# A state-space scan whose states are stored by half, chunk and run: neighbours in every step, real and imaginary rows swapped by ScalarE, four doubling steps in place of fifteen, single buffers

## The chip, the cores and the metric

One core of a Trainium2 chip runs the whole layer as one program. The metric is the device time of one execution, in microseconds (us); lower is better.

## What is computed

The reference is one hybrid decoder layer for 1024 positions of width 2048, all in 32-bit floats:

```python
h = rms_norm(x, norm_w)
q, k, v, a_gate, u, z, g_a, g_s = split(h @ w_in)
y_a = (sliding_window_attention(q, k, v, sinks) * silu(a_gate)) @ w_attn_proj
y_ssm = gelu(s5_ssm(u))                     # 64 groups of 16 channels, 64 complex states each
glu_a, glu_b = split(y_ssm @ w_glu + b_glu)
y_s = (glu_a * sigmoid(glu_b) * silu(z)) @ w_ssm_proj
x = x + (sigmoid(g_a) * y_a + sigmoid(g_s) * y_s) @ w_out
```

Inside `s5_ssm` a group's state follows s(t) = a s(t-1) + B u(t), with a complex diagonal a for each group, and y = Re(C s) + D u. This recurrence over 1024 positions is the scan that the change rewrites.

## The kernel before

Most of the program is matrix products on TensorE. Each weight tile of 128 x 1024 is loaded through SP's queue, split by ScalarE into a rounded high part `whi` and by VectorE into a rest `wlo` (`split`, lines 80 to 82), and used in `proj` (lines 110 to 127): 16 matmuls on `whi`, then 8 on `wlo`. These 24 matmuls are called a chunk below. The weight buffers `raw`, `whi` and `wlo` are two deep, so a late split of one chunk holds the loads and splits of the next ones.

Beside this main work run side jobs, written as Python generators. `drive` takes one step of the main job, then `pull` takes steps of the side jobs at a given rate. That fixes the program's order; a scheduler with its own timeline then sets the order of instructions on each engine, which is fixed when the program is built. Every engine works strictly through its own queue.

The scan is the side job `ssm` (lines 656 to 763), spawned at line 1180 beside the gate and sigmoid projections. 1024 positions are 128 blocks of 8, and the state is carried from block to block. Groups are taken in four batches of 16 (`bt`). In a batch:

- Loads bring the block inputs `uq` and the tables for B; GpSimd multiplies these into `bm` (lines 696 to 701), TensorE makes the block contributions `px` (line 706), and ScalarE copies them into `X` (line 708), once for each half `q` of 8 groups.
- `X` holds for every group 128 blocks and one zero in front. Real parts are in partitions 0 to 63, imaginary parts in 64 to 127. VectorE scans it with `step` (lines 713 to 725): one step is `xo += al*xi + be*swap(xi)`, and the swap of halves is made by two 64-row multiplications that read the other half (lines 722 and 723). So a step is five instructions.
- There are three parts. In 16 runs of 8 blocks, 7 steps go along each run, on 16 x 16 values whose neighbours lie 8 elements apart. Then 15 steps in sequence carry the run ends, on 16 values each. Then two steps spread each run's start over its 7 other blocks, 840 values each.
- GpSimd makes the output table `ct` (`ctable`, lines 438 to 452), `tz` is loaded, TensorE multiplies both with `uq` and `X` into `py` (lines 753 and 754), ScalarE applies GELU, and 16 stores write the result.

`uq`, `X`, `ct`, `c1`, `c2`, `v1` and `v2` have two buffers each, and `tz` one of its own, so that parts of the next batch can start while the present one is scanned. The power tables `p1`, `p2`, `al`, `be` are made in `ssm_prep` at the start and read once for all groups (lines 673 to 675).

The order of positions in a block row is set where `uproj` writes `ut` (lines 203 to 206), and undone in `glu` (line 959).

```python
tt(v1, xi, a, mul)
tt(v2[0:64], xi[64:128], b[64:128], mul)
tt(v2[64:128], xi[0:64], b[0:64], mul)
tt(v1, v1, v2, add)
tt(xo, xo, v1, add)
```

Of the kernel before, what the change touches and what calls it, by code (L numbers as in the profile page):

```python
# [32 lines left out]
def _build(nc, tc, I, OUT, ctx):  # L33
# [24 lines left out]
    PTD = dp.tile([4, 128, 9, NG], F32, name="ptd")  # L58
# [162 lines left out]
    for kt in range(KT):  # L221
# [5 lines left out]
        x = b0.tile([128, TH], F32, tag="x0", bufs=10, name="x0")  # L227
# [210 lines left out]
    def ctable(bp, tt, eng, p1, p2, g0, ng):  # L438

        shp = [128, ng, 9, 16]  # L440
        ct = bp.tile([128, 8, 9, 16], F32, tag="ct", bufs=2, name="ct")
# [1 line left out]
        c1 = bp.tile([128, ng, 16], F32, tag="c1", bufs=2, name="c1")
        c2 = bp.tile([128, ng, 16], F32, tag="c2", bufs=2, name="c2")
# [9 lines left out]
    def ssm_prep(bp, pp):  # L454
# [160 lines left out]
        al, be = tl((128, 9, NG), "al"), tl((128, 9, NG), "be")  # L615
# [40 lines left out]
    def ssm(bp, pp):  # L656
# [6 lines left out]
        def ts(o, a, s1, s2=None, op0=ALU.mult, op1=ALU.add):  # L663
            if s2 is None:
                V.tensor_scalar(o, a, s1, None, op0=op0)
            else:
# [4 lines left out]

        mul, add, sub = ALU.mult, ALU.add, ALU.subtract
        p1, p2, al, be = (tl((128, 9, NG), n) for n in ("p1", "p2", "al", "be"))
        for n, t in enumerate((p1, p2, al, be)):
            nc.sync.dma_start(t, PTD[n])
        for bt in range(4):
            gs = bt * GB
            uq = tl((128, GB, NCH), "uq", 2)
# [3 lines left out]
            X = tl((128, GB, NCH + 1), "X", 2)  # L682
            V.memset(X[:, :, 0:1], 0.0)

            for q in range(2):
# [16 lines left out]
                for qq in range(2):  # L702
# [5 lines left out]
                    S.copy(X[:, q * 8 + qq * 4:q * 8 + qq * 4 + 4, 1:NCH + 1], px)  # L708
                yield

            X4 = X[:, :, 1:NCH + 1].rearrange("p g (s k) -> p g s k", k=8)

            def step(xo, xi, a, b, shp):
                n = math.prod(shp)
                v1 = tl((128, 840), f"v1{bt % 2}")[:, 0:n]
                v2 = tl((128, 840), f"v2{bt % 2}")[:, 0:n]
                if len(shp) == 2:
                    v1, v2 = (v.rearrange("p (a b) -> p a b", a=shp[0]) for v in (v1, v2))
                elif len(shp) == 3:
                    v1, v2 = (v.rearrange("p (a b c) -> p a b c", a=shp[0], b=shp[1]) for v in (v1, v2))  # L720
# [587 lines left out]
```

## Time and profile before

| | |
|---|---|
| median of 3 runs (lowest to highest) | 2611.91 us (2608.07 to 2616.03) |
| the profiled execution, its span | 2613.01 us, 2611.2 us |
| TensorE matmuls busy | 2480.6 us, 95% of the span |
| VectorE busy | 1654.7 us, 63% |
| ScalarE busy | 916.9 us, 35% |
| GpSimd busy | 917.3 us, 35% |
| mean granted TensorE clock | 0.981 of full speed |

Shares of the whole span hide the stages. The scan lies between about 860 and 1460 us of the span, and it is read by windows of that stretch: for each window the busy time of each engine and the granted clock (1.00 is 2.4 GHz, 0.5 is 1.2 GHz).

### The profile page before, as it was taken

What the parts mean: (1) busy time and instruction counts of PE and PEld (TensorE: products, weight loads), DVE (VectorE), ACT (ScalarE), POOL (GpSimd) and SP (SyncE); (2) the same over time, 40 slices, a digit from 0 to 9 for tenths busy, and PEclk for the clock granted to TensorE, in tenths of its full rate; (3) what the DMA queues carried; (4) which work ended last, traced back from release to release, by engine and by line L of the source; (5) the groups of instructions that cost most, each with busy time, mean ns of one, the idle gap of its engine ahead of it and who ended that gap; (6) DMA issues with size and microseconds to landing.
All of it is one profiled execution on the core that took longest, in us unless ns stands there. A gap on an engine that the chain in (4) does not pass through costs nothing. (4 is left out here: it accounts for less than half of the span.)

```text
span 2611.2 us, 30785 instructions
## 1 busy us (share of the span) xinstructions
PE 2480.6 (95%) x11012; PEld 2016.8 (77%) x11012; DVE 1654.7 (63%) x2294; ACT 916.9 (35%) x1378; POOL 917.3 (35%) x715
## 2 busy tenths in 40 slices
PE   7999999999999998899999989999999999899997
PEld 5878887788878777787777868887877877678886
DVE  7995557984776287948586243226687686744542
ACT  5332454453666223131332232223352231233311
POOL 4110014350444534132120230004547656514466
PEclk9999999999999998999999999999999999999999
DMA  6543343223333745445464674336358677797765
GB/s 206 191 139 109 96 141 105 84 83 97 97 95 103 217 129 135 152 129 157 133 168 135 210 259 156 121 121 202 120 191 282 211 257 234 246 313 270 226 218 181
DMA packets 195609, 438.55 MB, mean 168 GB/s; under 512 B 41312, under 2 KB 53632, under 8 KB 195456
## 3 DMA queue, kind: packets, MB, share of 16 engines
q1 hardware_dynamic: 159680, 344.14, 43.6%
q0 software_dynamic: 19504, 63.08, 6.4%
q10 hardware_dynamic: 16272, 29.38, 2.9%
q8 instruction: 86, 1.41, 0.2%
q14 instruction: 67, 0.55, 0.1%
HBM read 341.73 MB, written 94.77 MB: 167 GB/s over the span
## 5 line engine op out<-in xcount | busy, mean ns | idle before, releaser
L121 PE MATMUL ps<-hh,whi 128*128 128x512 f32 x2144 | 851.3, 397 | 13.7 <-ACT whi L81 9.7
L122 PE MATMUL ps<-hl,whi 128*128 128x512 f32 x2144 | 844.5, 394 | 0.8 <-DVE hl L144 0.8
L82 DVE TENSOR_TENSOR wlo<-wraw,whi 128x1024 fp32r<-128x1024 f32 (+1 forms) x344 | 448.6, 1306 | 455.3 <-ACT whi L81 216.9
L125 PE MATMUL ps<-hh,wlo 128*128 128x512 f32 x2144 | 549.8, 396 | 32.0 <-DVE wlo L82 32.0
L81 ACT CAST whi<-wraw 128x1024 fp32r<-128x1024 f32 (+1 forms) x344 | 348.4, 1014 | 627.4 <-PE ps L122 301.3
L125 PEld LDWEIGHTS ps<-hh,wlo 128*128 128x128 f32 x2144 | 404.7, 190 | 124.6 <-DVE wlo L82 39.5
L121 PEld LDWEIGHTS ps<-hh,whi 128*128 128x128 f32 x2144 | 407.2, 190 | 108.5 <-ACT whi L81 17.1
L122 PEld LDWEIGHTS ps<-hl,whi 128*128 128x128 f32 x2144 | 407.1, 190 | 86.7 <-DVE hl L144 2.1
L82 DVE TENSOR_TENSOR wlo<-ws,whi 128x1024 fp32r<-128x1024 f32 x80 | 118.9, 1488 | 127.1 <-ACT whi L81 93.7
L81 ACT CAST whi<-ws 128x1024 fp32r<-128x1024 f32 x80 | 84.0, 1051 | 307.5 <-POOL ws L856 116.7
L856 POOL TENSOR_TENSOR ws<-wraw 128x512 f32<-128x512 f32 (+1 forms) x72 | 136.5, 1896 | 135.6 <-DVE wlo L82 103.3
L421 POOL TENSOR_TENSOR pa<-ph,c_mct 128x512 fp32r<-128x512 f32 x32 | 43.1, 1347 | 253.8 <-ACT ph L81 253.6
L178 POOL DMA_DIRECT2D gsd<-sg x32 | 17.5, 547 | 274.9 <-ACT sg L177 274.9
L177 ACT ACTIVATE sg<-sg 128x512 f32<-128x512 f32 x64 | 40.5, 632 | 198.1 <-DVE sg L176 198.0
L661 DVE TENSOR_TENSOR v<-X,be 64x16 f32<-64x16 f32 (+2 forms) x192 | 91.9, 479 | 2.8
L402 ACT ACTIVATE scs<-scs,m,rq 128x128 f32<-128x128 f32 x128 | 61.8, 484 | 63.9 <-DVE m L396 63.9
L1001 POOL TENSOR_TENSOR mt<-mt,pa 128x512 f32<-128x512 f32 x32 | 57.0, 1782 | 76.9 <-DMA pa<-pd 24.3
L178 POOL DMA_DIRECT2D gd<-sg x32 | 17.8, 556 | 170.6 <-ACT sg L177 163.5
L862 PE MATMUL psm<-q4h,whi 128*128 128x512 f32 x160 | 67.6, 422 | 4.0 <-DVE mt L996 2.7
L862 PE MATMUL psm<-q1h,whi 128*128 128x512 f32 x160 | 64.4, 403 | 6.1 <-ACT whi L81 6.1
L863 PE MATMUL psm<-q4l,whi 128*128 128x512 f32 x160 | 66.2, 414 | 0.0
L862 PE MATMUL psm<-q2h,whi 128*128 128x512 f32 x160 | 62.6, 392 | 3.1 <-ACT qa L893 3.1
(343 smaller groups left out, 4187.8 us busy)
## 6 DMA issues: line engine op xcount, KB each, us to landing
wraw<-w_in SPq DMA_DIRECT2D x268, 512.0 KB, 3.6
wraw<-w_out SPq DMA_DIRECT2D x72, 512.0 KB, 5.2
x<-xT SPq DMA_DIRECT2D x96, 256.0 KB, 4.0
gd<-sg POOLq DMA_DIRECT2D x32, 256.0 KB, 3.9
gsd<-sg POOLq DMA_DIRECT2D x32, 256.0 KB, 2.9
wraw<-w_glu SPq DMA_DIRECT2D x16, 512.0 KB, 4.3
wraw<-w_attn SPq DMA_DIRECT2D x16, 512.0 KB, 5.1
sga<-gd SPq DMA_DIRECT2D x32, 256.0 KB, 4.3
```

The lines of the kernel that those rows point to most:

```text
L81: S.copy(hi, src)
L82: V.tensor_tensor(lo, src if src2 is None else src2, hi.bitcast(F32), op=ALU.subtract)
L121: PE.matmul(ps, hi[:, kk, :], rh[kt], start=(kt == 0), stop=False)
L122: PE.matmul(ps, hi[:, kk, :], rl[kt], start=False, stop=False)
L125: PE.matmul(ps, lo[:, kk, :], rh[kt], start=False, stop=(kt == last))
L402: S.activation(sc[:, r, :], sc[:, r, :], AF.Exp, bias=m4[:, r:r + 1], scale=RQ[h, p][:, b, 2 * r + e:2 * r + e + 1], accum_out=den[:, r:r ...
L421: G.tensor_tensor(a, ph.bitcast(F32), mb, op=ALU.mult)
L661: (eng or V).tensor_tensor(o, a, b, op=op)
L856: G.tensor_tensor(o, a, b, op=ADD)
L862: PE.matmul(ps, hi[:, c0 + k, :], rh, start=(first and k == 0), stop=False, skip_group_check=True)
L863: PE.matmul(ps, hi[:, c0 + k, :], rl, start=False, stop=False, skip_group_check=True)
L1001: G.tensor_tensor(t, t, p, op=ADD)
```

## The change

Positions inside a half of 512 are reordered from (run and chunk, position) so that for a fixed chunk k of a run the 8 runs s of that half lie side by side. `X` becomes (group, half, 9 chunks, 8 runs); chunk 0 holds the state with which a run starts. `step` copies its input with the two halves of partitions exchanged into `xs` with two ScalarE copies, and VectorE then has four instructions over all 128 partitions. The run ends are gathered into `E`, and four steps with distances 1, 2, 4 and 8 replace the fifteen; for them `al` and `be` get three more powers, squared one from another in `ssm_prep`, which takes `x0` from 10 to 9 buffers. The power tables are loaded for each batch. `uq`, `X`, `ct`, `c1`, `c2`, `v1`, `v2` have one buffer; `tz` is loaded by halves into the buffer of `bm`, and `E` takes the buffer of `bmu`.

```diff
-            raw = b0.tile([128, TH], F32, tag="x0", bufs=10, name="ur")
+            raw = b0.tile([128, TH], F32, tag="x0", bufs=9, name="ur")
...
-            src = ps.rearrange("p (c j) -> p j c", j=8)
-            V.tensor_tensor(ut, src, rstd[h].rearrange("p (c j) -> p j c", j=8), op=ALU.mult)
+            order = lambda t: t.rearrange("p (s k j) -> p j k s", k=8, j=8)
+            V.tensor_tensor(ut.rearrange("p j (k s) -> p j k s", k=8), order(ps), order(rstd[h]), op=ALU.mult)
...
-        al, be = tl((128, 9, NG), "al"), tl((128, 9, NG), "be")
+        al, be = tl((128, 12, NG), "al"), tl((128, 12, NG), "be")
...
+        for n in (9, 10, 11):
+            p = slice(n - 1, n)
+            cmul(al[:, n:n + 1, :], be[:, n:n + 1, :], al[:, p, :], be[:, p, :], al[:, p, :], be[:, p, :],
+                 u1[:, 0:1, 0:NG])
...
-            uq = tl((128, GB, NCH), "uq", 2)
+            p1, p2, al, be = (tl((128, 9 if n < 2 else 12, GB), t) for n, t in enumerate(("p1", "p2", "al", "be")))
+            for n, t in enumerate((p1, p2, al, be)):
+                nc.sync.dma_start(t, PTD[n, :, 0:9 if n < 2 else 12, gs:gs + GB])
+            uq = tl((128, GB, NCH), "uq", 1)
...
-            X = tl((128, GB, NCH + 1), "X", 2)
+            X = tl((128, GB, 2, 9, 8), "X", 1)
...
-                tt(v1, xi, a, mul)
-                tt(v2[0:64], xi[64:128], b[64:128], mul)
-                tt(v2[64:128], xi[0:64], b[0:64], mul)
+                S.copy(m[0:64], xi[64:128])
+                S.copy(m[64:128], xi[0:64])
+                tt(v1, bc(xi), a, mul)
+                tt(v2, bc(m), b, mul)
                 tt(v1, v1, v2, add)
                 tt(xo, xo, v1, add)
...
-            for s in range(1, 16):
-                step(X4[:, :, s, 7], X4[:, :, s - 1, 7], al[:, 8, gs:gs + GB], be[:, 8, gs:gs + GB], (GB,))
+            E = tl((128, GB, 1, 16), "bmu", name="E")
+            S.copy(E.rearrange("p g o (h s) -> p (g o) h s", h=2), X[:, :, :, 8, :])
+            for n, d in enumerate((1, 2, 4, 8)):
+                bc = lambda x: x[:, 8 + n, :].unsqueeze(2).unsqueeze(3).to_broadcast([128, GB, 1, 16 - d])
+                step(E[:, :, :, d:16], E[:, :, :, 0:16 - d], bc(al), bc(be), (GB, 1, 16 - d))
+            S.copy(X[:, :, 0, 0, 1:8], E[:, :, 0, 0:7])
+            S.copy(X[:, :, 1, 0, :], E[:, :, 0, 7:15])
...
-            tz = tl((128, GB, 128), "tz", 1)
+                tz = tl((128, 8, 128), "bm", 1, name="tz")
...
-                G.tensor_tensor(o.rearrange("p (c i) -> p i c", i=8), g.rearrange("p (i c) -> p i c", i=8),
-                                z.rearrange("p (c i) -> p i c", i=8), op=MUL)
+                back = lambda t: t.rearrange("p (s k i) -> p i k s", k=8, i=8)
+                G.tensor_tensor(back(o), g.rearrange("p (i k s) -> p i k s", i=8, k=8), back(z), op=MUL)
```

How the built order moves is shown at three places. The first is VectorE in the steps along the runs of the first batch, from one weight split to the next (L82 is the split, L661 and L665 are the scan, `v` is `v1` or `v2`). Before:

```order
L82 TENSOR_TENSOR wlo<-wraw,whi 128x1024
L661 TENSOR_TENSOR v_7552<-X,al 128x256
L661 TENSOR_TENSOR v_7553<-X,be 64x256 x2
L661 TENSOR_TENSOR v_7552<-v_7552,v_7553 128x256
L661 TENSOR_TENSOR X<-X,v_7552 128x16x16
L661 TENSOR_TENSOR v_7589<-X,al 128x256
L661 TENSOR_TENSOR v_7590<-X,be 64x256 x2
L661 TENSOR_TENSOR v_7589<-v_7589,v_7590 128x256
L82 TENSOR_TENSOR wlo<-wraw,whi 128x1024
```

Now:

```order
L82 TENSOR_TENSOR wlo<-wraw,whi 128x1024
L665 TENSOR_TENSOR v_7613<-X,al 128x256
L665 TENSOR_TENSOR v_7614<-xs,be 128x256
L665 TENSOR_TENSOR v_7613<-v_7613,v_7614 128x256
L665 TENSOR_TENSOR X<-X,v_7613 128x32x8
L665 TENSOR_TENSOR v_7657<-X,al 128x256
L665 TENSOR_TENSOR v_7658<-xs,be 128x256
L665 TENSOR_TENSOR v_7657<-v_7657,v_7658 128x256
L665 TENSOR_TENSOR X<-X,v_7657 128x32x8
L82 TENSOR_TENSOR wlo<-wraw,whi 128x1024
```

About two steps stand between two weight splits in both; a step has four instructions in place of five.

The second is ScalarE in the same stretch (L81 makes `whi`, L705 copies `px` into `X`, L715 and L716 are the swaps, L177 is a sigmoid). Where before only L81 and L177 stand there, it is now:

```order
L705 COPY X<-px 128x8x64 x2
L715 COPY xs<-X 64x256
L716 COPY xs<-X 64x256
L81 CAST whi<-wraw 128x1024
L715 COPY xs<-X 64x256
L716 COPY xs<-X 64x256
L177 ACTIVATE sg<-sg 128x512
L715 COPY xs<-X 64x256
L716 COPY xs<-X 64x256
L81 CAST whi<-wraw 128x1024
```

Each cast of a weight tile now stands behind one or two pairs of swaps, and each pair waits for VectorE's step before it.

The third is GpSimd where the first batch ends and the second begins (`ct`, `ctu`: output table; `bm`, `bmu`: input table; L193 issues a store). Before:

```order
L661 TENSOR_TENSOR ct<-ct,ctu 128x1152
L661 TENSOR_TENSOR ctu<-c_10294,p_7277 128x1152
L661 TENSOR_TENSOR bm<-pwr,bre 128x8x64
L661 TENSOR_TENSOR bm<-pwr,bim 128x8x64
L661 TENSOR_TENSOR bm<-bm,bmu 128x8x64
L661 TENSOR_TENSOR bmu<-pwi,bre 128x512
L661 TENSOR_TENSOR bm<-bm,bmu 128x8x64
L193 DMA agd_75<-sg 128x512
```

Now:

```order
L665 TENSOR_TENSOR bm<-pwr,bre 128x8x64
L665 TENSOR_TENSOR bm<-pwr,bim 128x8x64
L665 TENSOR_TENSOR ct<-c_9031,p_8212 128x1152
L665 TENSOR_TENSOR bm<-bm,bmu 128x8x64
L665 TENSOR_TENSOR ct<-ct,ctu 128x1152
L193 DMA agd_75<-sg 128x512
L665 TENSOR_TENSOR bmu<-pwi,bre 128x512
L665 TENSOR_TENSOR ctu<-c_9117,p_8213 128x1152
L665 TENSOR_TENSOR bm<-bm,bmu 128x8x64
```

All of the rows shown second wait for the last `py` product of the first batch, since `tz` sits in the buffer of `bm`.

## Rows read from the trace of the kernel before

**Rows 1.** Who TensorE waited for, 860 to 1460 us: total, times, longest.
```profile
PE ps L125 <- DVE wlo L82: 29.3, 14, 4.8
PE px L706 <- POOL bm L661: 13.0, 2, 6.5
```
**Rows 2.** Busy time by stretch: PE, PEld, DVE, ACT, POOL, granted clock, DMA share, GB/s.
```profile
860.00:1415.00 555.00, 505.90 (x2282) 413.50 (x2281) 390.52 (x656) 151.55 (x181) 159.76 (x114) 0.96 0.54 151
900.00:925.00 25.00, 21.86 (x96) 18.69 (x97) 8.80 (x6) 6.54 (x8) 23.77 (x15) 0.86 0.71 226
925.00:1005.00 80.00, 73.12 (x329) 58.33 (x328) 73.98 (x139) 17.24 (x21) 16.09 (x13) 0.98 0.35 111
1030.00:1060.00 30.00, 23.48 (x99) 19.63 (x98) 23.20 (x27) 7.92 (x9) 13.04 (x9) 0.83 0.79 203
1060.00:1130.00 70.00, 61.41 (x252) 48.76 (x251) 62.20 (x127) 14.56 (x17) 9.58 (x12) 0.95 0.46 143
1300.00:1330.00 30.00, 25.97 (x122) 21.03 (x122) 16.94 (x19) 12.55 (x19) 13.35 (x8) 0.89 0.74 170
1570.00:1640.00 70.00, 70.00 (x310) 57.98 (x310) 20.39 (x21) 18.00 (x20) 4.27 (x8) 1.00 0.43 143
```
**Rows 3.** VectorE's groups by form, 860 to 1460 us: busy, mean ns of one.
```profile
L82 DVE TENSOR_TENSOR wlo<-wraw,whi 128x1024 fp32r<-128x1024 f32 x89 | 128.8, 1448 | 155.2 <-ACT whi L81 91.6 <-PE ps L125 52.4 <-DMA c<-sC 7.0
L661 DVE TENSOR_TENSOR v<-X,be 64x256 f32<-64x256 f32 x56 | 44.3, 790 | 0.8
L661 DVE TENSOR_TENSOR v<-X,be 64x840 f32<-64x840 f32 x16 | 26.6, 1661 | 0.4
L661 DVE TENSOR_TENSOR X<-X,v 128x256 f32<-128x256 f32 x28 | 22.3, 797 | 0.8
L661 DVE TENSOR_TENSOR v<-X,be 64x16 f32<-64x16 f32 x120 | 21.1, 176 | 1.7
L661 DVE TENSOR_TENSOR v<-X,al 128x256 f32<-128x256 f32 x28 | 20.5, 732 | 7.1 <-ACT X L708 6.5
...
L661 DVE TENSOR_TENSOR v<-v,v 128x256 f32<-128x256 f32 x28 | 14.2, 506 | 0.6
L661 DVE TENSOR_TENSOR v<-X,al 128x840 f32<-128x840 f32 x8 | 12.9, 1614 | 0.2
...
L661 DVE TENSOR_TENSOR X<-X,v 128x840 f32<-128x840 f32 x8 | 8.2, 1030 | 0.2
```
**Rows 4.** VectorE in order of time: start, length; the same addition twice.
```profile
932.62 1.34 DVE L661 TENSOR_TENSOR v<-v,v 128x256 f32<-128x256 f32 x1
...
939.68 0.43 DVE L661 TENSOR_TENSOR v<-v,v 128x256 f32<-128x256 f32 x1
```
**Rows 5.** GpSimd in order of time, the same microseconds.
```profile
932.12 1.56 POOL L661 TENSOR_TENSOR bm<-pwr,bim 128x512 f32<-128x512 f32 x1
...
937.14 1.46 POOL L661 TENSOR_TENSOR bm<-bm,bmu 128x512 f32<-128x512 f32 x1
```
**Rows 6.** ScalarE's groups by form: small and cross-partition copies, up to 1640 us.
```profile
L404 ACT ACTIVATE es<-es 128x4 f32<-128x4 f32 x32 | 6.1, 190 | 0.0
...
L312 ACT CAST kh<-kk 64x512 fp32r<-64x512 f32 x4 | 2.5, 618 | 0.1
```
**Rows 7.** GpSimd's groups by form, 860 to 1640 us.
```profile
L661 POOL TENSOR_TENSOR bm<-bm,bmu 128x512 f32<-128x512 f32 x16 | 25.4, 1587 | 0.5
L661 POOL TENSOR_TENSOR ct<-ct,ctu 128x1152 f32<-128x1152 f32 x8 | 21.6, 2694 | 0.4
L661 POOL TENSOR_TENSOR ctu<-c,p 128x1152 f32<-128x1152 f32 x8 | 21.0, 2627 | 0.4
```
**Rows 8.** VectorE's groups by form, whole span: a product with broadcast operands.
```profile
L459 DVE TENSOR_TENSOR ct<-c,p 128x1152 f32<-128x1152 f32 x8 | 10.7, 1342 | 0.0
```
**Rows 9.** Busy time by stretch, 100 to 200 us.
```profile
100.00:200.00 100.00, 100.00 (x496) 79.91 (x495) 93.23 (x131) 31.89 (x42) 14.16 (x24) 1.00 0.47 145
```
**Rows 10.** The product with z in the GLU: count, least, median and greatest ns, first and last start.
```profile
L959 POOL TENSOR_TENSOR s<-ga,z x16: 1651/2049/2123, 1815.3 to 1957.9; 128x512 f32<-128x512 f32 x16
```

More of the change, by code (lines that the diff above doesn't have):

```diff
@@ L57, in _build @@
     PWD = dp.tile([2, 8, NG, 64], F32, name="pwd")
-    PTD = dp.tile([4, 128, 9, NG], F32, name="ptd")
+    PTD = dp.tile([4, 128, 12, NG], F32, name="ptd")
     KD = dp.tile([16, NG, 256], F32, name="kd")
@@ L226, in _build @@
             w[n, 1] = load_w(win(12 + n)[1], 2, *spare[n])
-        x = b0.tile([128, TH], F32, tag="x0", bufs=10, name="x0")
+        x = b0.tile([128, TH], F32, tag="x0", bufs=9, name="x0")
         nc.sync.dma_start(x, I["xT"][kt, :, 0:TH])
@@ L435, in attention_block, with ctable @@
         yield
[L438 removed]
+    def ctable(bp, tt, eng, p1, p2, g0, ng, at, bufs):
         shp = [128, ng, 9, 16]
[L441 removed]
+        ct = bp.tile([128, 8, 9, 16], F32, tag="ct", bufs=bufs, name="ct")
         u = bp.tile([128, 8, 9, 16], F32, tag="ctu", bufs=1, name="ctu")
[L443 to L444 removed]
+        c1 = bp.tile([128, ng, 16], F32, tag="c1", bufs=bufs, name="c1")
+        c2 = bp.tile([128, ng, 16], F32, tag="c2", bufs=bufs, name="c2")
         nc.sync.dma_start(c1, I["sC1"][:, g0:g0 + ng, :])
@@ L707, in ssm @@
                                   uq[:, q * 8 + gg, :], start=True, stop=True)
-                    S.copy(X[:, q * 8 + qq * 4:q * 8 + qq * 4 + 4, 1:NCH + 1], px)
+                    S.copy(X[:, q * 8 + qq * 4:q * 8 + qq * 4 + 4, :, 1:9, :].rearrange("p g h k s -> p g h (k s)"),
+                           px.rearrange("p g (h c) -> p g h c", h=2))
                 yield
-            X4 = X[:, :, 1:NCH + 1].rearrange("p g (s k) -> p g s k", k=8)
             def step(xo, xi, a, b, shp):
                 n = math.prod(shp)
[L715 to L720, printed above, removed]
-                tt(v1, xi, a, mul)
-                tt(v2[0:64], xi[64:128], b[64:128], mul)
-                tt(v2[64:128], xi[0:64], b[0:64], mul)
+                v1, v2 = (tl((128, 896), t)[:, 0:n].rearrange("p (a b c) -> p a b c", a=shp[0], b=shp[1])
+                          for t in ("v1", "v2"))
+                m = tl((128, 256), "xs")[:, 0:math.prod(xi.shape[1:])]                     .rearrange("p (a b c) -> p a b c", a=shp[0], b=xi.shape[2])
+                S.copy(m[0:64], xi[64:128])
+                S.copy(m[64:128], xi[0:64])
+                bc = lambda x: x if x.shape[2] == shp[1] else x.to_broadcast([128] + list(shp))
+                tt(v1, bc(xi), a, mul)
+                tt(v2, bc(m), b, mul)
                 tt(v1, v1, v2, add)
@@ L735, in ssm @@
-            for q in range(2):
-                shp = [128, 8, 15, 7]
-                gl = slice(q * 8, q * 8 + 8)
-                bc = lambda x: x.rearrange("p k g -> p g k")[:, gs + q * 8:gs + q * 8 + 8, 1:8] \
-                    .unsqueeze(2).to_broadcast(shp)
-                step(X4[:, gl, 1:16, 0:7], X4[:, gl, 0:15, 7:8].to_broadcast(shp), bc(al), bc(be), shp[1:])
-                yield
-            tz = tl((128, GB, 128), "tz", 1)
-            for j in range(8):
-                nc.sync.dma_start(tz[16 * j:16 * j + 16], KD[:, gs:gs + GB, 128 - 16 * j:256 - 16 * j])
@@ L746, in ssm @@
-            for q in range(2):
-                ct = ctable(bp, tt, G, p1, p2, gs + q * 8, 8)
+            E = tl((128, GB, 1, 16), "bmu", name="E")
[3 more added lines that the diff above has]
+                step(E[:, :, :, d:16], E[:, :, :, 0:16 - d], bc(al), bc(be), (GB, 1, 16 - d))
+                if n % 2:
+                    yield
@@ new lines, in ssm @@
+            S.copy(X[:, :, 0, 0, 1:8], E[:, :, 0, 0:7])
+            S.copy(X[:, :, 1, 0, :], E[:, :, 0, 7:15])
+            for h in range(2):
+                bc = lambda x: x.rearrange("p k g -> p g k")[:, :, 1:8].unsqueeze(3).to_broadcast([128, GB, 7, 8])
+                step(X[:, :, h, 1:8, :], X[:, :, h, 0:1, :], bc(al), bc(be), (GB, 7, 8))
+                yield
+            for q in range(2):
+                tz = tl((128, 8, 128), "bm", 1, name="tz")
+                for j in range(8):
+                    nc.sync.dma_start(tz[16 * j:16 * j + 16],
+                                      KD[:, gs + q * 8:gs + q * 8 + 8, 128 - 16 * j:256 - 16 * j])
+                ct = ctable(bp, tt, G, p1, p2, gs + q * 8, 8, q * 8, 1)
```

31 lines of the change are left out of this document (10 added, 21 removed).

## The prediction
> **What bounds the kernel now.** I read the stretch of the scan, not the page's shares. Over 860 to 1415 us TensorE's matmuls are busy 505.9 of 555 us and the granted clock averages 0.96 [rows 2]; so 49.1 us are idle and 0.04 x 555 = 22.2 us go to the lower clock level, 1.2 GHz. The list of TensorE's waits says for whom [rows 1]: 29.3 us, in 14 pieces, for VectorE's weight split `wlo`, and 13.0 us, in two pieces of 6.5, for GpSimd's input table `bm`. The rest is small.
>
> Why a weight split is late is read from the windows. From 925 to 1005 us, the first batch's scan, VectorE is busy 74.0 us [rows 2]. TensorE loses 80 - 73.1 = 6.9 us to idling and 0.02 x 80 = 1.6 to the clock, so its matmuls needed 71.5 us. VectorE had more to do than TensorE (103%). From 1060 to 1130 it is 62.2 us against 70 - 8.6 - 3.5 = 57.9 (107%). Two-deep weight buffers hide the first microseconds of such a lag; then TensorE waits once per chunk. **In the scan VectorE is the bound; elsewhere TensorE is.**
>
> I call the two places where a batch begins joints. They show the same wait and then a slower clock: in 900 to 925 us 0.14 x 25 = 3.5 us and in 1030 to 1060 us 0.17 x 30 = 5.1 us go to the clock [rows 2]. With the two waits of 6.5 us [rows 1] the joints cost 10.0 and 11.6 us, together 21.6. The window 1300 to 1330 us, where inputs are rebuilt, takes 0.11 x 30 = 3.3 us of clock loss and stays as it is. What is left of the clock loss, 22.2 - 3.5 - 5.1 - 3.3 = 10.3 us, belongs to the waits on `wlo`. **The scan costs 29.3 + 10.3 = 39.6 us.**
>
> **VectorE's scan.** Before, one step along the runs costs 0.732 + 2 x 0.790 + 0.506 + 0.797 = 3.62 us and there are 28: 101.2 us. The chain over run ends is 60 steps of five instructions of about 0.176: 52.8 us. The spread is eight steps of 1.614 + 2 x 1.661 + 2 x 1.030 = 7.00 (the sum of the two products, not shown, taken as the last addition): 56.0 us [rows 3]. Together 210 us.
>
> After, every instruction covers 128 partitions and reads runs of eight neighbours. Rows bound the price. Elements that lie 8 apart make the 128x256 addition 0.797 us; the contiguous one is 0.506, and at 840 elements in runs of seven neighbours it is 1.030, 1.2 ns per element where the former is 3.1 [rows 3]. Broadcast operands do not slow a product: 1152 elements in 1.342 us, 1.2 ns each [rows 8]. So I take the contiguous price, 0.506 at 256 elements and 0.0009 us for each further one. Steps along runs: 28 x 4 x 0.506 = 56.7 us. Doubling steps have 240, 224, 192 and 128 elements, 196 on average, 0.453 us: 16 x 4 x 0.453 = 29.0. Spread, 896 elements, 1.08: 8 x 4 x 1.08 = 34.6. Together 120 us, **90 us less**. If all went at the strided price it would be about 28 x 4 x 0.797 + 16 x 4 x 0.797 + 8 x 4 x 1.66 = 193 us, 17 less; that is the upper bound.
>
> There is a lower one. The same 128x256 addition took 1.34 us at 932.6, while GpSimd was multiplying tables, and 0.43 at 939.7, after GpSimd's last one had ended at 938.6 [rows 4, 5]. In the new order the tables of the next batch stand at the joint and no longer in the scan. At 0.43 the steps along runs cost 48.2 us, the doubling steps 24, and all about 105.
>
> The Trainium skill (SBUF — State Buffer, "Who interferes with whom") says that a VectorE instruction with two inputs in SBUF and a GpSimd instruction that reads SBUF take turns on one read interface. By that rule the forecast would be the fourth case below, with the scan at 0.43; the two rows agree with it.
>
> **What the swaps add.** ScalarE gets 104 swaps (two for each of 28 + 16 + 8 steps) and 12 copies around `E`. No row shows a 64x256 copy between halves; a 64x512 one takes 0.618 and a 4-element instruction 0.190 [rows 6]. In between lie 0.40 at 256, 0.36 at 196 and 0.30 at 128: 56 x 0.40 + 32 x 0.36 + 16 x 0.30 + 12 x 0.40 = 44 us (22 to 72 at the ends). ScalarE is busy 151.6 of 555 us [rows 2], so the room is there. What counts is order: VectorE waits for the second swap, having only the first product (0.51) to do meanwhile: 0.80 - 0.51 = 0.3 us for each of 52 steps, 16 us. Behind a waiting swap stand the casts that make `whi` (second excerpt of the order); they can come late by what is left of VectorE's step, some 1.4 us, and a weight buffer gives more than that.
>
> So a batch's scan takes (120 + 16) / 4 = 34 us of VectorE's time in place of 52.5. In the first batch that leaves 74.0 - 22.5 + 4 = 55.5 us, and since the scan now runs beside some ten chunks instead of thirteen or fourteen, about four weight splits fewer fall into it: near 49 us. A chunk needs 24 x 70.0 / 310 = 5.4 us of TensorE [rows 2], ten need 54. The load falls from 103 to about 91%. Two thirds of the scan's cost should go; I keep a third, 13 us, since the splits still stand behind two steps each. **Gain 27 us** (bounds: nothing, and all 39.6).
>
> **What single buffers add.** The next batch's `bm` may start only when the last `py` product has read `tz`. From there to `px` GpSimd has five table products of `bm`, two of `ct` and one of `ctu` (third excerpt, nine rows): 5 x 1.59 + 2 x 2.69 + 2.63 = 16.0 us [rows 7], and an issue of a store. The scheduler left 83 matmuls between them, 83 x 0.226 = 18.7 us. That holds by a little; I take 3 us for each of the three later joints. The first has no predecessor and stays at 10.0. Between the two halves of a batch `tz` is loaded again and `ct` made again: 2 us in each of four batches. `py` now waits for the end of a shorter scan right behind it: 1 us in each. Sum 10 + 9 + 8 + 4 = 31 us, against 21.6: **9 us lost**. No row of before shows the last two. Their bounds are nothing and the 6.5 us wait [rows 1] each time.
>
> **Costed at nothing.** Three more squarings in the preparation, 18 instructions, at most 18 x 0.506 = 9 us of VectorE, in a stretch where TensorE never idles [rows 9]; VectorE is busy 93% there, so if that cover went, some of the 9 us would show. Nine `x0` buffers: the last input tile's matmuls move behind 16 others that are ready earlier. The table loads are 12 more transfers, the `tz` loads 32 more, on SP's queue, where each weight load stands behind them; they fall into the joint terms. The product with z reads and writes with a wider stride, 2.05 us now [rows 10]; sixteen of them at 0.797 / 0.506 of that would add 19 us to GpSimd, which is not the bound there. After the scan the order of all engines is otherwise the same, so I expect the same times there.
>
> **Sum.** 2613.0 (profiled) - 27 + 9 = 2595. The median of the runs is 1.1 lower: **2594 us**.
>
> **The rivals.** *The gain is eaten.* Swaps slower than 0.4 us, or products at the strided price, leave VectorE at 100% and over in the scan: of 39.6 us some 30 stay, and with 9 lost at the joints it comes to 2612. For: the price of a swap is interpolated. Against: ten chunks leave 5 us of room.
>
> *Slower.* The later joints decide. If GpSimd's chain there exceeds 18.7 us, because it stands behind a store that waits for a late gate product, TensorE runs dry as in 1030 to 1060: 11.6 us each time instead of 3, also at the four reloads of `tz`. Seven times 11.6 is 81, plus the first 10.0, against 21.6: 70 lost, 27 gained, 2655; with half of them 2618 to 2635. For: exactly this wait stands there twice in the present trace. Against: 2.7 us of room.
>
> The Trainium skill (Trainium Kernel Development and Optimization, "Best Practices") advises double buffers so that transfers overlap with work. By that rule this case would be the likeliest; the two waits of 6.5 us arose with double buffers, so they do not bear it out.
>
> *Larger gain.* The scan free of GpSimd's tables at 0.43 and joints that hold: 2613.0 - 39.6 - 11.6 = 2562, less 1.1: 2561.
>
> **Chances.** Forecast 0.58 (2578 to 2603), larger gain 0.12, eaten 0.17, slower 0.13. A measurement of this kernel tells 0.3%, about 8 us, from no change; so faster means under 2604, slower over 2620. The range runs from 2564, into the larger gain, to 2619, over the eaten one, and leaves out the slower case and the end of the larger. Faster 0.71, same 0.17, slower 0.12.
>
> **What would show it.** Right: VectorE's scan near 120 us in four forms of about 0.45 to 0.5 and 1.1 us; TensorE's wait on `wlo` in this stretch under 15 us; its waits on `bm`, `tz` and `X` near 20. Wrong: products at 0.73 or more, swaps at 0.6, or waits of 5 us at every joint; or a gain that comes from outside 860 to 1460 us.

## The result and the profile after

The changed kernel takes 2546.29 us (median of 4 runs, 2542.53 to 2552.07), the kernel before on the same chip 2609.99 (2606.82 to 2616.03): a ratio of 0.9755, interval 0.9728 to 0.9783. It is faster by 64 us where 18 were forecast, and its time lies 18 us under the forecast range.

The profiled execution's span fell from 2611.2 to 2540.8 us. Busy time by stretch shows where (us; PE, PEld, DVE, ACT, POOL, granted clock, DMA share, GB/s). The kernel before, from the start of the stage to the same piece of work behind it (3873 and 3868 matmuls):

```profile
0.00:860.00 860.00, 836.07 (x3810) 675.10 (x3811) 629.06 (x966) 416.39 (x749) 252.79 (x225) 0.99 0.38 120
...
860.00:1785.00 925.00, 863.22 (x3873) 708.24 (x3871) 512.50 (x782) 252.99 (x300) 223.58 (x192) 0.97 0.53 158
```

The changed kernel:

```profile
0.00:860.00 860.00, 839.52 (x3814) 676.94 (x3815) 629.99 (x985) 418.00 (x749) 253.99 (x226) 0.99 0.38 120
...
860.00:1719.00 859.00, 842.19 (x3868) 700.17 (x3866) 413.01 (x509) 297.02 (x412) 227.04 (x192) 0.99 0.56 170
...
1719.00:2541.00 822.00, 777.49 (x3332) 630.00 (x3332) 514.52 (x548) 248.73 (x332) 440.47 (x299) 0.98 0.69 231
```

The preparation takes as long as before. The stage is 66 of the 70 us shorter: TensorE idles 16.8 us instead of 61.8, and its matmuls take 842.2 instead of 863.2 us, because the clock averages 0.99 instead of 0.97.

Who TensorE waited for from 860 to 1720 us in the changed kernel (total, times, longest), beside [rows 1]:

```profile
PE px L703 <- POOL bm L665: 9.3, 5, 3.4
PE ps L121 <- ACT whi L81: 4.7, 3, 4.2
PE ps L125 <- DVE wlo L82: 1.7, 1, 1.7
PE ps L122 <- DVE hl L144: 1.0, 1, 1.0
```

The waits for `wlo` are gone but for one of 1.7 us, and the single buffers did not lengthen those for `bm`. VectorE's and ScalarE's groups by form, 860 to 1400 us, beside [rows 3, 6]:

```profile
L82 DVE TENSOR_TENSOR wlo<-wraw,whi 128x1024 fp32r<-128x1024 f32 x88 | 130.3, 1481 | 147.0 <-PE ps L125 87.5 <-ACT whi L81 39.5 <-DMA yd<-yt 16.6
...
L665 DVE TENSOR_TENSOR X<-X,v 128x256 f32<-128x256 f32 x28 | 11.9, 423 | 0.8
L665 DVE TENSOR_TENSOR v<-v,v 128x256 f32<-128x256 f32 x28 | 11.8, 423 | 0.7
L665 DVE TENSOR_TENSOR v<-xs,be 128x256 f32<-128x256 f32 x28 | 11.8, 423 | 12.8 <-ACT xs L716 12.7
...
L665 DVE TENSOR_TENSOR v<-X,al 128x896 f32<-128x896 f32 x8 | 11.0, 1380 | 0.1
```
```profile
L715 ACT COPY xs<-X 64x256 f32<-64x256 f32 x28 | 11.4, 407 | 20.2 <-DVE X L665 19.8
```

An operation of a run step costs 0.423 us; VectorE's scan takes 106.0 us in all, 210.8 before.

The rows that explain the result are VectorE's weight splits (L82) inside the four batches' scans, from a scan's first operation to its last (us; DVE busy, count; clock, DMA share, GB/s). Before:

```profile
929.00:1002.00 73.00, 13.07 (x9) 0.98 0.31 102
1042.00:1120.00 78.00, 13.48 (x11) 0.94 0.48 153
1182.00:1254.00 72.00, 12.26 (x10) 0.96 0.44 138
1327.00:1402.00 75.00, 14.64 (x12) 0.98 0.52 141
```

In the changed kernel:

```profile
921.00:967.00 46.00, 9.76 (x8) 1.00 0.51 146
1033.00:1083.00 50.00, 10.98 (x9) 1.00 0.58 161
1148.00:1195.00 47.00, 11.42 (x9) 1.00 0.52 146
1262.00:1319.00 57.00, 12.21 (x10) 1.00 0.56 178
```

TensorE uses up a split in 5.42 us (24 matmuls, [rows 2]). Before, 42 splits stand in 298 us: 70 us more than the 228 that they feed. Now 36 stand in 200 us and feed 195. I call this difference the excess of a window.

A window is also stretched by the waits that fall into it, so its excess alone does not tell cause from effect. VectorE's busy time does. The sums over the same four windows, all instructions, before and in the changed kernel:

```profile
sum 298.00, PE 266.20 PEld 211.50 DVE 283.07 ACT 59.41 POOL 45.76; mean PE 66.55 PEld 52.87 DVE 70.77 ACT 14.85 POOL 11.44
```
```profile
sum 200.00, PE 199.97 PEld 165.05 DVE 169.01 ACT 98.52 POOL 13.80; mean PE 49.99 PEld 41.26 DVE 42.25 ACT 24.63 POOL 3.45
```

Before, VectorE worked 283 us beside splits that feed TensorE for 228; now it works 169 us beside splits that feed it for 195.

### The profile page after: what moved, and what is told of

Same layout as the page of the kernel before. It is cut to its first block, busy times and chain, and to the rows that moved or that the text cites. A ratio compares the mean times of both kernels' runs of the same rounds, so it can differ in the third digit from the quotient of the medians.

```text
span 2540.8 us, 30817 instructions
## 1 busy us (share of the span) xinstructions
PE 2459.2 (97%) x11012; PEld 2007.1 (79%) x11012; DVE 1557.5 (61%) x2040; ACT 963.8 (38%) x1492; POOL 921.5 (36%) x715
## 5 line engine op out<-in xcount | busy, mean ns | idle before, releaser
L82 DVE TENSOR_TENSOR wlo<-wraw,whi 128x1024 fp32r<-128x1024 f32 (+1 forms) x344 | 445.2, 1295 | 488.9 <-PE ps L125 247.7
L81 ACT CAST whi<-wraw 128x1024 fp32r<-128x1024 f32 (+1 forms) x344 | 349.8, 1018 | 637.2 <-PE ps L122 372.0
L125 PE MATMUL ps<-hh,wlo 128*128 128x512 f32 x2144 | 542.0, 391 | 1.7 <-DVE wlo L82 1.7
L81 ACT CAST whi<-ws 128x1024 fp32r<-128x1024 f32 x80 | 84.2, 1054 | 292.5 <-POOL ws L855 80.4
L82 DVE TENSOR_TENSOR wlo<-ws,whi 128x1024 fp32r<-128x1024 f32 x80 | 116.4, 1456 | 115.7 <-ACT whi L81 74.4
L178 POOL DMA_DIRECT2D gsd<-sg x32 | 17.8, 556 | 226.7 <-ACT sg L177 214.8
L177 ACT ACTIVATE sg<-sg 128x512 f32<-128x512 f32 x64 | 40.6, 634 | 136.5 <-DVE sg L176 136.4
L402 ACT ACTIVATE scs<-scs,m,rq 128x128 f32<-128x128 f32 x128 | 62.2, 487 | 61.9 <-DVE m L396 61.8
L1000 POOL TENSOR_TENSOR mt<-mt,pa 128x512 f32<-128x512 f32 x32 | 56.3, 1762 | 74.9 <-DMA sgs<-gsd 22.6
L178 POOL DMA_DIRECT2D gd<-sg x32 | 17.7, 555 | 177.7 <-ACT sg L177 165.3
L862 PE MATMUL psn<-q3l,whi 128*128 128x512 f32 x160 | 62.8, 393 | 1.6 <-DVE q3l L82 1.6
```

Of the source, the lines that this page charges most:

```text
L81: S.copy(hi, src)
L82: V.tensor_tensor(lo, src if src2 is None else src2, hi.bitcast(F32), op=ALU.subtract)
L125: PE.matmul(ps, lo[:, kk, :], rh[kt], start=False, stop=(kt == last))
L402: S.activation(sc[:, r, :], sc[:, r, :], AF.Exp, bias=m4[:, r:r + 1], scale=RQ[h, p][:, b, 2 * r + e:2 * r + e + 1], accum_out=den[:, r:r ...
L862: PE.matmul(ps, hi[:, c0 + k, :], rl, start=False, stop=False, skip_group_check=True)
L1000: G.tensor_tensor(t, t, p, op=ADD)
```

## The experiments

The kernel before was measured again with every set of experiments and took 2610 to 2614 us each time; ratios and their intervals are against it. The changed kernel's 0.9755 of that is 2546 to 2550. Theory A, at first: TensorE loses in proportion to VectorE's scan time. Waits are counted over the whole stage, where those for `wlo` were 32.0 us before. Three dots stand for lines left out of an edit.

**The swaps by VectorE again.**

```diff
-                S.copy(m[0:64], xi[64:128])
-                S.copy(m[64:128], xi[0:64])
...
-                tt(v2, bc(m), b, mul)
+                tt(v2[0:64], bh(xi[64:128]), b[64:128], mul)
+                tt(v2[64:128], bh(xi[0:64]), b[0:64], mul)
```

The sign in the table `be` moves to its other half with this.

> The changed kernel, but the halves are swapped by VectorE again: the product with be is two products of 64 partitions, and ScalarE's two copies per step are gone. VectorE's scan work goes from 106.0 us to about 132 (28 more of 0.42 us, 16 more of 0.29 to 0.40, 8 more of 1.09). Theory A (what TensorE loses in the stage follows VectorE's scan time, 61 us for the 104.8 that it fell by, so 0.58 us per us): 15 us slower than the changed kernel, 2561 us. Theory B (VectorE has slack and only above a threshold does it lose): within 5 us of the changed kernel, 2543 to 2551. Theory C (the gain came from the rearranged ends of the batches, their buffers and tables, not from VectorE's time): 2546 too, waits on wlo as few as now.

Measured 2551.08 us, 0.9751 (0.9728 to 0.9775), with VectorE's scan at 134.2 us: 28 us more work, at no cost that shows. The swaps on ScalarE brought nothing that shows. Theory A's straight line, which asked for 15 us, falls.

**A chain of 15 in place of doubling.**

```diff
-            for n, d in enumerate((1, 2, 4, 8)):
...
-                step(E[:, :, :, d:16], E[:, :, :, 0:16 - d], bc(al), bc(be), (GB, 1, 16 - d))
...
+            for s in range(1, 16):
...
+                step(E[:, :, :, s:s + 1], E[:, :, :, s - 1:s], bc(al), bc(be), (GB, 1, 1))
```


> The changed kernel, but the four doubling steps are a chain of 15 steps over one column each (16 elements per partition). VectorE's scan work goes up by about 20 us (23 out, 240 operations of 0.18 in = 43), ScalarE gets 88 more copies, and each batch's chain is some 10 us longer. Theory A (0.58 us per us of VectorE): 12 us slower, 2558 us. Theory B (threshold): 2543 to 2551. Theory D (it is the length of the chain, through the order of the joints, that counts, not the load): batches' joints later by 10 us each, 2560 to 2585 with waits of TensorE on px, py or X rather than on wlo.

Measured 2559.12 us, 0.9788 (0.9762 to 0.9813), some 9 us slower than the changed kernel. Waits for `wlo` 1.4 us, for `bm` 15.1 (9.3 there), for `whi` 9.5 (4.7). VectorE's load (127.2 us) does not make the splits late; the longer chain costs mostly at the joints, a little less than theory D asked for. The time alone would fit theory A as well (2558); the waits do not.

**X strided, same order.**

```diff
-            X = tl((128, GB, 2, 9, 8), "X", 1)
+            X = tl((128, GB, 2, 8, 9), "X", 1).rearrange("p g h s k -> p g h k s")
```

ScalarE's copy of `px` into `X` becomes two copies with this, one for each half.

> The changed kernel with the same instructions of VectorE in the same order, but X is laid out so that a step's states lie 9 elements apart instead of side by side. The run steps' two operations that touch X go from 0.42 us to 0.73 and 0.80 (rows of the kernel before), so VectorE's scan work rises by about 21 us to 127. If the price of a stride is the reason for the cheaper steps, X<-X,v of 256 is again near 0.80 us here; if not, it stays at 0.42. Time by theory A: 12 us slower, 2558; by B or C: 2543 to 2551.

Measured 2568.52 us, 0.9831 (0.9798 to 0.9865). Some 19 us slower, but not for the reason expected. VectorE's and TensorE's groups by form:

```profile
L665 DVE TENSOR_TENSOR X<-X,v 128x256 f32<-128x256 f32 x28 | 18.3, 654 | 0.8
```
```profile
L754 PE MATMUL py<-X,ct 128*128 128x128 f32 x128 | 39.3, 402 | 5.2 <-DVE X L665 5.1
```

The stride does cost VectorE (0.654 against 0.423 us; 131.9 us of scan), yet waits for `wlo` stay at 1.8 us. What costs most is TensorE's own read of `X`: 128 matmuls of 0.402 in place of 0.275 us, 15.2 us more. Waits for `X` add 5.1 us and those for `bm` 4.0 (13.3 against 9.3); the second copy has a share in these that was not taken apart.

**The single buffers alone, on the kernel before.**

```diff
-            uq = tl((128, GB, NCH), "uq", 2)
+            uq = tl((128, GB, NCH), "uq", 1)
...
-            X = tl((128, GB, NCH + 1), "X", 2)
+            X = tl((128, GB, NCH + 1), "X", 1)
...
-            tz = tl((128, GB, 128), "tz", 1)
+                tz = tl((128, 8, 128), "bm", 1, name="tz")
```

In the same way `ct`, `c1`, `c2`, `v1` and `v2` are single, and `p1`, `p2`, `al`, `be` are loaded per batch.

> The kernel before with the buffers of the changed one alone: uq, X, ct, c1, c2 and v single, tz in two halves in the tag of bm, the tables p1, p2, al and be loaded per batch; the scan itself as before (210.8 us of VectorE). Theory C (the ends of the batches brought the gain): 2550 to 2580. Theories A and B: no gain, 2605 to 2625, wlo waits as before (about 30 us), with 0 to 10 us more for px waiting on bm.

Measured 2591.04 us, 0.9906 (0.9878 to 0.9934): 23 us faster, which A excludes, and less than C asked for. Its run steps got cheaper without an edit to them (beside [rows 3]):

```profile
L661 DVE TENSOR_TENSOR v<-X,be 64x256 f32<-64x256 f32 x56 | 35.7, 638 | 0.8
...
L661 DVE TENSOR_TENSOR X<-X,v 128x256 f32<-128x256 f32 x28 | 19.6, 699 | 0.7
```

0.638 in place of 0.790 us. Before, GpSimd built the next batch's `bm` beside the first run steps ([rows 4, 5]); with `tz` in that buffer it cannot. Waits for `wlo` fall to 17.4 us. This led to theory E, that GpSimd's tables at the joints were what hurt.

**More work for VectorE in the changed kernel.** Two and four more products in every step.

```diff
 tt(v2, bc(m), b, mul)
+tt(v2, bc(m), b, mul)
+tt(v1, bc(xi), a, mul)
```


> Half of that dose: two more operations in every step, VectorE's scan work about 159 us. Theory A': still mostly hidden, 2550 to 2565. Theory E: 2546 to 2553. A straight line by VectorE's time (0.58 us per us, which the swap run spoke against): 2580.

> The changed kernel with four more VectorE operations in every step (the two products twice more each, same result), so that VectorE's scan work is about 212 us, what the kernel before had (210.8), while layout, ScalarE's swaps, doubling, buffers and GpSimd's tables stay. Theory A' (VectorE's scan time costs only above what the stage can hide; 134 us was still hidden, 211 is not): waits on wlo return, 20 to 40 us slower than the changed kernel, 2570 to 2590. Theory E (what hurt in the kernel before was GpSimd's tables at the joints, beside the first run steps and ahead of bm, not VectorE's load): within 10 us of the changed kernel, 2546 to 2560, hardly a wait on wlo.

The large dose: 2544.28 us, 0.9749 (0.9728 to 0.9770). **206 us of scan, as much as before within 5, cost nothing.** The small one: 2566.46 us, 0.9833 (0.9806 to 0.9860), slower than both, with 1.3 us of waits for `wlo` but 14.4 for `bm` and 6.9 behind loads at a `py`; so this loss lies at the joints, which the small dose happened to place worse. Theory A is out. The splits inside the scans of the large dose:

```profile
921.00:1004.00 83.00, 18.29 (x15) 1.00 0.49 141
1071.00:1148.00 77.00, 17.09 (x14) 1.00 0.48 141
1215.00:1315.00 100.00, 21.92 (x18) 1.00 0.60 178
1383.00:1464.00 81.00, 18.30 (x15) 1.00 0.40 123
```

62 splits in 341 us feed 336. The sum over the same windows, all instructions:

```profile
sum 341.00, PE 339.35 PEld 280.06 DVE 309.30 ACT 136.24 POOL 21.20; mean PE 84.84 PEld 70.02 DVE 77.33 ACT 34.06 POOL 5.30
```

The order gives each batch some 15 splits instead of some 10, so VectorE's 309 us stand beside 336 of TensorE's, not 283 beside 228 as before, and TensorE hardly idles. From this, **theory F: TensorE waits for what a scan's window exceeds the splits in it times 5.42 us, less a lead.** The lead, about 9 us, is fitted to the kernel before: its finer windows (73.3, 77.6, 71.9, 74.9 us, with 10, 11, 10 and 12 splits; the tenth of the first starts as that scan ends) exceed by 19.1, 18.0, 17.7 and 9.9, less 9 each 28.7; measured 29.3 [rows 1].

**Buffers again.** All of the former ones double in the changed kernel (`tz` in a tag of its own); then, in a second kernel, `bm` double too, the last pair of lines; and, in the kernel before, `ct`, `c1`, `c2` alone single (edit not shown).

```diff
-            uq = tl((128, GB, NCH), "uq", 1)
+            uq = tl((128, GB, NCH), "uq", 2)
...
-            X = tl((128, GB, 2, 9, 8), "X", 1)
+            X = tl((128, GB, 2, 9, 8), "X", 2)
...
-                bm = tl((128, 8, 2, 64), "bm", 1)
+                bm = tl((128, 8, 2, 64), "bm", 2)
```


> The changed kernel with the double buffers back: uq, X, ct, c1, c2, v1, v2 and the four small tables double, tz in a tag of its own. Theory E: GpSimd's ct tables move back to the joints, between the two halves of bm and beside the first run steps; px waits longer (13 us and more instead of 9), a few run steps cost twice, and the 23 us that single buffers gave the kernel before are lost in part: 2556 to 2575. Theory A' (with VectorE's load at 106 us nothing is lost by that): 2546 to 2555.

> The changed kernel with double buffers for uq, X, ct, c1, c2, v1, v2 and the small tables, tz in its own tag, and bm double as well: GpSimd can build a batch's second bm while the first is in use, so px's waits (9 us in the changed kernel, 3.7 with the double buffers but single bm) fall below 3 us, while some tables move beside the run steps, whose windows grow by under 10 us per batch, which the lead still hides (theory F): 2536 to 2546, level with the changed kernel or up to 8 us faster. Theory E: slower than it by 5 to 15 us, 2552 to 2562.

> The kernel before with one edit: in the scan ct, c1 and c2 have one buffer instead of two, so that GpSimd can't build the second table of a batch before the first is used. Theory E: this is where the 23 us of the single buffers come from; 2590 to 2598 (on a chip where the kernel before takes 2614), run steps at 0.64 to 0.70 us instead of 0.79, px waits fewer. Rival: it was the single uq and X, the halved tz or the tables per batch: 2608 to 2618.

Measured 2544.65 us, 0.9749 (0.9728 to 0.9770): level with the changed kernel, though `v<-xs,be` rises from 0.423 to 0.584 us beside GpSimd. With `bm` double 2554.20, 0.9787 (0.9772 to 0.9801): some 10 us worse, which is theory E's range and not F's 2536 to 2546; waits for `wlo` are 3.3 us there, for `tz` 3.6 and for `bm` 4.9. `ct` alone 2605.79, 0.9974 (0.9959 to 0.9989): 6 us, not the 23. Theory E falls as the whole story: contention comes back in the first of these and costs nothing.

**tz in bm's buffer alone, on the kernel before.**

```diff
-            tz = tl((128, GB, 128), "tz", 1)
...
+                tz = tl((128, 8, 128), "bm", 1, name="tz")
```


> The kernel before with one edit: tz in two halves in the buffer of bm, so that GpSimd can't build the next batch's bm before the last py of this one, as it does in the kernel before beside the first run steps. Theory F: the run steps cost 0.64 to 0.70 us instead of 0.79, the windows' excess falls by some 5 us per batch as with all the single buffers together, and most of their 23 us is here: 2588 to 2600. Rival (it was the other buffers or the tables per batch): 2605 to 2618.

Measured 2599.94 us, 0.9962 (0.9947 to 0.9977): 10.5 of the 23 us; the run steps' two strided operations at 0.656 and 0.662 us, waits for `wlo` 17.8. So the fewer waits for `wlo` come with this edit alone; it brings less time because 13.6 us of other waits, for loads ahead of `py`, appear. If the edits add up, `ct` has 6 of the 23 us, and some 6 stay unassigned.

**Neighbours alone, on the kernel before.** Run steps on 16 neighbouring columns, all else in its place.

```diff
-                step(X4[:, :, :, k], X4[:, :, :, k - 1], bc(al), bc(be), (GB, 16))
+                step(X[:, :, 16 * k + 1:16 * k + 17], X[:, :, 16 * k - 15:16 * k + 1], bc(al), bc(be), (GB, 16))
```


> The kernel before, where the run steps read and write 16 neighbouring columns of X per group instead of 16 columns that lie 8 apart (it leaves out the right choice of states: the recurrence runs over other columns). The order of TensorE, ScalarE, GpSimd and SP is the kernel before's, row for row, and VectorE's too but for a few neighbours swapped. Theory F (in the order a batch's scan stands beside some 10 weight conversions, which TensorE uses up in 10 x 5.42 us; it waits for what the scan's window is longer than that, less a lead of about 9 us): each batch's window falls by the stride's price, 7 x (2 x 0.37 + 0.31 + 0.37) = 10 us, so the windows' excess of 19, 18, 18 and 10 us becomes about 9, 8, 8 and 0, waits on wlo fall from 32 to under 8 us, clock with them: 25 to 40 us faster than the kernel before, 2572 to 2588 where that takes 2612. Theory E (contention with GpSimd at the joints was what hurt): 5 to 12 us faster, 2600 to 2607.

Measured 2596.05 us, 0.9945 (0.9930 to 0.9960): 14 us, where F forecast 25 to 40. The sign is right, the size was off:

```profile
L661 DVE TENSOR_TENSOR X<-X,v 128x256 f32<-128x256 f32 x28 | 15.2, 543 | 0.8
```
```profile
PE ps L125 <- DVE wlo L82: 16.1, 11, 2.3
```

Beside GpSimd's tables the neighbours cost 0.543, not 0.42. The windows exceed by 13.4, 14.2, 13.4 and 3.5 us; less 9 each 14.0, against 14.4 measured up to 1460 us (the other 1.7 lie behind the scans).

**Neighbours and single buffers, on the kernel before.** Both edits above.

> The kernel before with both: the single buffers (tz in bm, tables per batch) and run steps on 16 neighbouring columns (which leaves out the right choice of states). Theory F: without GpSimd beside them the run steps fall to about 0.43 us, 7 x (2 x 0.21 + 0.22 + 0.27) = 6.4 us per batch below the single buffers alone, whose windows' excess was 12.6, 14.1, 11.0 and 6.9 us; so 6, 8, 5 and 0, all under the lead: wlo waits under 4 us instead of 17, 12 to 20 us faster than single buffers alone, 2571 to 2580 where the kernel before takes 2612. What is then left to the changed kernel (25 to 30 us) are the joints and the stage behind the scan. Theory A (a line by VectorE's time, 1 us per us): the same sign, 2565.

Measured 2569.14 us, 0.9829 (0.9799 to 0.9860): 43 us, 2 us below F's range. The two edits apart gave 14 and 23, and the intervals don't tell their sum from 43.

```profile
L661 DVE TENSOR_TENSOR X<-X,v 128x256 f32<-128x256 f32 x28 | 11.9, 424 | 0.7
```
```profile
PE px L706 <- POOL bm L661: 8.4, 3, 3.5
PE py L754 <- DMA tz<-kd: 7.8, 1, 7.8
PE ps L121 <- ACT whi L81: 7.3, 2, 3.7
PE ps L122 <- DVE hl L144: 5.3, 3, 1.9
PE py L754 <- DMA p<-ptd: 2.8, 1, 2.8
PE ps L125 <- DVE wlo L82: 2.6, 3, 1.3
```

With stride and contention both gone the operation costs what it costs in the changed kernel, and the waits for `wlo` are gone with it. Some 21 us are left to the changed kernel. The waits in which the two differ are 10.6 us for loads ahead of `py` (`tz` and the tables), 4.3 for `hl` and 2.6 for `whi`; of the remaining edits, doubling is worth some 9 us by the chain of 15, the swaps nothing that shows.

**The kernel before without its scan.**

```diff
-                step(X4[:, :, :, k], X4[:, :, :, k - 1], bc(al), bc(be), (GB, 16))
...
-                step(X4[:, :, s, 7], X4[:, :, s - 1, 7], al[:, 8, gs:gs + GB], be[:, 8, gs:gs + GB], (GB,))
...
-                step(X4[:, gl, 1:16, 0:7], X4[:, gl, 0:15, 7:8].to_broadcast(shp), bc(al), bc(be), shp[1:])
...
+            for _ in range(12):
                 yield
```


> The kernel before without the scan's steps (it leaves the recurrence out; VectorE has 0 instead of 211 us of it). Theory F: no window, so no wait on wlo in the stage; px's waits at the joints stay (10 to 15 us) and so do those behind the scan (1490 to 1570 us): 35 to 50 us faster than the kernel before, 2562 to 2577, no better than the changed kernel, which has its scan. If the changed kernel's gain were all from a lighter scan, this would be faster than the changed kernel.

Measured 2548.70 us, 0.9760 (0.9741 to 0.9779), 62 us where F forecast 35 to 50. **The scan cost the kernel before 62 us, and the changed kernel, with its scan, is as fast as one without.** Its waits:

```profile
PE ps L121 <- ACT whi L81: 9.4, 5, 4.1
PE px L706 <- POOL bm L661: 6.5, 1, 6.5
PE ps L121 <- ACT hh L143: 1.8, 1, 1.8
PE ps L125 <- DVE wlo L82: 1.8, 1, 1.8
```

One of the two waits of 6.5 us for `bm` is gone too, and the slower clock behind it; both go with the scan:

```profile
1030.00:1060.00 30.00, 27.74 (x121) 22.33 (x120) 15.72 (x15) 7.26 (x9) 10.31 (x9) 1.00 0.64 196
```

**The pace alone, on the kernel before.** First ScalarE copies in the run steps (four pairs, in a weaker one two), which give the order more splits per batch:

```diff
                 tt(v1, v1, v2, add)
+                if len(shp) == 2:
...
+                    for _ in range(4):
+                        S.copy(m, v1)
+                        S.copy(v1, m)
                 tt(xo, xo, v1, add)
```


> The kernel before with nothing made cheaper: in each run step eight ScalarE copies of 128x256 (the sum copied to and fro, same result) stand between the third and the fourth VectorE operation. VectorE's scan work stays at 211 us, ScalarE gets 224 copies of about 0.4 us (90 us) more, and the order now puts about 15 weight conversions instead of 10 beside each batch's scan; the joints (px, py) stand in the same places of TensorE's order. Theory F (TensorE waits for what a batch's window exceeds its conversions x 5.42 us, less about 9): windows of 80 to 90 us against 15 x 5.42 = 81, excess under 9 us, wlo waits under 6 us instead of 32: 25 to 45 us faster than the kernel before, 2566 to 2586 where that takes 2611. Theory A (VectorE's load in all, or the strides themselves): no gain or slower, 2608 to 2640. Theory G (the length of the chain): slower, 2615 to 2650.

> Half of that: four ScalarE copies per run step, 13 conversions in the order beside a batch's scan. Theory F: windows of some 75 us against 13 x 5.42 = 70, excess 5 to 10 us, wlo waits of 3 to 10 us in all: 20 to 40 us faster than the kernel before, 2571 to 2591. Theories A and G: 2608 to 2630.

Measured 2611.84 us, 1.0001 (0.9983 to 1.0019), and 2596.10, 0.9942 (0.9925 to 0.9958). Both are misses, 0 and 16 us where F forecast 25 to 45 and 20 to 40. Waits for `wlo` halve (15.6 and 17.0 us), but those for `whi` rise to 15.6 and 18.3 (9.7 before). In the weaker dose the windows grow to some 87 us with 13 or 14 splits, and VectorE, which stands behind the copies, is busy 303 of their 349 us. They exceed by 61 us in all, and by F `wlo` alone should wait 25; F's sum does not hold here. Then VectorE work that waits for nothing:

```diff
+                if len(shp) == 2:
...
+                    for _ in range(4):
+                        tt(m, v1, v2, add)
                 tt(v1, v1, v2, add)
```


> The kernel before with four more VectorE additions of 128x256 on neighbours in every run step (into a tile that nobody reads, same result): VectorE's scan work goes from 211 to about 260 us. The order now puts 13 to 16 weight conversions instead of 10 beside a batch's scan; px and py stand in the same places of TensorE's order. Theory F (what counts is the time VectorE needs per conversion that the order puts beside the scan; the added work brings its own conversions): the windows' excess stays or falls, 2595 to 2618 where the kernel before takes 2612. Theory A (TensorE's loss grows with VectorE's scan time, 0.58 us per us): 2635 to 2645.

Measured 2604.98 us, 0.9964 (0.9952 to 0.9977), with VectorE's scan at 266.8 us. **56 us more work made the kernel 9 us faster.** Waits for `wlo` 19.6 us. The windows, 94.8, 100.6, 87.8 and 94.8 us, hold 13, 16, 14 and 16 splits. The first exceeds by more than before (24.4 in place of 19.1), the others by less (13.9, 12.0 and 8.1 in place of 18.0, 17.7 and 9.9). Waits for `bm` fall to 6.6 us and 7.3 for `X` appear.

**How far theory F goes.** Of its eight forecasts of a time two held (`tz` in the buffer of `bm`, and the added work); six missed. Taken on each run's own windows, its sum stands beside the measured waits for `wlo` up to 1460 us, in the kernel before and five edits of it that add no work, as 28.7 to 29.3, 27.1 to 25.3 (`ct` alone), 10.8 to 16.0 (single buffers), 11.9 to 15.4 (`tz` alone), 14.0 to 14.4 (neighbours) and 1.7 to 1.3 (both). With added work it is too high: 23.3 to 17.8, and 25.2 to 14.7 with the weaker copies. So it ranks the kernels by their waits for `wlo`, with one fitted number; it does not give their times, because the joints move with every order.

## Why the prediction was wrong

**VectorE's part: right.** That VectorE was the bound in the scan, and would no longer be, is what the windows show (283 us of work beside 228, now 169 beside 195). Its scan was forecast at 120 us with 105 as the lower end; 106.0 measured. The lower end's reason was the right one: 0.423 us where GpSimd is not beside it, as the 0.43 of [rows 4] said, and 0.543 with neighbours but with GpSimd (the neighbours run) against 0.424 without (the run with both edits). The Trainium skill (SBUF — State Buffer, "Who interferes with whom") states this contention; these two runs agree with it. A swap took 0.407 us against 0.40. One of the four spread operations was mispriced, 1.380 us against 1.08 (`v<-X,al`, 896 elements).

**"I keep a third, 13 us": wrong.** The waits for `wlo` inside the scans fell to nothing; the one left, 1.7 us, lies at 1414 us, behind them, and the clock is 1.00 in all four. The prediction's own working had 49 us of VectorE's work beside ten splits that feed 54, which is no excess at all; the third had no row behind it. That is 13 us. What decides is VectorE's work against the splits that the order sets beside it, not its load in all: 206 us of scan with 15 splits a batch cost nothing in the changed kernel, 211 with 10 cost the kernel before 62.

**"9 us lost" at the joints: wrong.** They were forecast at 31 us, after 21.6. Waits for `bm` went from 13.0 to 9.3 us, those for `X` and `tz` do not appear, and the clock falls at two joints only:

```profile
900.00:925.00 25.00, 21.43 (x102) 18.16 (x103) 11.28 (x12) 9.25 (x14) 13.03 (x10) 0.93 0.54 159
...
1245.00:1275.00 30.00, 26.40 (x116) 21.01 (x115) 24.74 (x30) 17.91 (x28) 10.73 (x7) 0.94 0.72 223
```

That is 0.07 x 25 + 0.06 x 30 = 3.6 us of clock, so the joints cost 12.9 us, 9 less than before. The rival made single buffers the slower ones. The Trainium skill (Trainium Kernel Development and Optimization, "Best Practices") advises double buffers. Here they changed nothing in the changed kernel (0.9749 against 0.9755), and in the kernel before the single ones were 23 us faster, in large part (10.5 us with `tz` alone) because they kept GpSimd's tables out of the run steps. The loss that did not come is 9 us.

**"The scan costs 29.3 + 10.3 = 39.6 us": wrong, and with it the bound of the gain.** I counted as the scan's only what waits for `wlo`. The kernel without scan shows 62. The other 22 us stood under other names. In the changed kernel 9 of them come back at the joints (in the kernel without scan one of the 6.5 us waits and its clock are gone); 6 at the rebuilding of inputs at 1300 us (4.0 us idle and 3.3 of clock, "stays as it is"; 1.0 us waited there now); and 6 in the stage behind the scan ("I expect the same times there": from 1460 to 1570 us 12.2 us were idle, now 6.4 from 1400 to 1465). The three steps give 13 + 9 + 22 = 44 of the 46 us missed. Why the stage behind the scan is better off was not taken apart: what stands in it moved with the order.

**The range.** It ended at 2564 because even the larger gain took 39.6 us for all that the scan could give back.

**The swaps** were costed at 16 us of VectorE's waits; 18.6 are there for `xs`, 12.7 of them in the run steps (rows above) and 5.9 in the doubling steps. VectorE doing them itself gives the same time, so they carried neither a gain nor a loss that shows.

## What to carry to other kernels

When one engine does side work in an order fixed ahead, compare the work of each stretch on that engine, at its real prices, with the time for which the main engine's inputs prepared inside it last, and not the engine's total load. Up to that line the inputs were not late in these runs, well above it they were; how many microseconds it costs depended on the joints as well. Before pricing what an edit can give back, run the kernel without that work: it shows waits that carry other names. A single buffer that holds back another engine can be the faster one, as it was in the kernel before.

## What the runs showed that was not expected

A matmul whose moving operand lies 9 elements apart took 0.402 instead of 0.275 us (`py<-X,ct`, 128 columns), as VectorE's addition took 0.654 instead of 0.423. Small differences in the order moved the joints by more than some edits cost: half a dose of added work was 22 us slower than the full dose.
